# A two-layer trunk of token mixers: the RWKV heads in units of one 128-channel tile, PSUM banks per stage, gate rows through DRAM

## The chip, the cores and the metric

The kernel runs on one core of one Trainium2 chip. The metric is the device time of one execution in microseconds (us); less is better. The core has TensorE (PE, the matrix engine, whose results go to PSUM, eight banks of 128 x 512 fp32), VectorE (DVE), ScalarE (ACT), GpSimd (POOL), and SyncE (SP), whose instruction stream issues all DMA transfers here. Each engine takes its own instructions in a fixed order and waits on semaphores for the others.

## What is computed

Two decoder layers on x (256 tokens x 2048 channels, fp32). Layer 0 mixes tokens with eight mLSTM heads of 128 channels and sixteen RWKV-7 heads of 64; layer 1 with retention and gated DeltaNet (GDN). Each layer has a mixer and a SwiGLU part, both as

```python
shift, scale, gate = _ada(c, ada_w[layer, 0], ada_b[layer, 0])   # silu(c) @ (2048 x 6144), in thirds
h = x * (1.0 + scale) + shift
y = _mixer_ab(h, ...)                       # layer 0; _mixer_cd in layer 1; _swiglu in the second half
x = _layer_norm(ALPHA * x + (1.0 + gate) * y, ln_g[layer, 0], ln_b[layer, 0])
```

The part that the change is about is the RWKV recurrence, for each head with a 64 x 64 state S:

```python
def step(S, inp):
    rt, wt, kt, vt, at, bt = inp                       # at = -kk, bt = kk * a
    sa = jnp.einsum('bhij,bhj->bhi', S, at)
    S = S * wt[:, :, None, :] + sa[..., None] * bt[:, :, None, :] + vt[..., None] * kt[:, :, None, :]
    return S, jnp.einsum('bhij,bhj->bhi', S, rt)
...
y = _head_norm(jnp.moveaxis(y, 0, 1), ln_g, ln_b, eps=RWKV_LN_EPS)
bonus = ((rh * kh * r_k.reshape(H, N)).sum(-1, keepdims=True) * vh).reshape(B, T, -1)
return ((y + bonus) * g).astype(z.dtype)
```

## The kernel before

The program is written in a tile framework: the Python code names tiles from pools, and a scheduler makes each engine's fixed order from program order, priorities, its own estimate of times, and free buffers. A tile is given out when one of its pool's buffers is free.

All large products go through `unit` (lines 360 to 362): a 1 MB block of fp32 weights is loaded into one of three `raw` buffers, ACT and DVE split it into a high and a low part (`split`, lines 340 and 341), and 24 matmuls of 512 columns follow, three for each exact product. `product` joins two to four such units into two of the four `g` banks. Between units, `fill` works off the modulation matrix: for each 1 MB piece of `ada` a DMA into a `raw` buffer and one DVE instruction (line 292). `ada_unit` collects the gates in `g1`; `gate_rows` (line 320) spreads them over 128 partitions with 16 matmuls against the identity, at each of four calls.

The stages in order: start (`first_products`, until about 165 us), RWKV, mLSTM, output product with layer norm (`mix_out`), SwiGLU (`ffn`), and the same for layer 1.

RWKV (`rwkv`) runs four batches of two 128-channel tiles (four heads). `rwkv_tiles` (708) turns a product's result (`zt`, two buffers) to channels by tokens, in `z` tiles (six buffers, three for each 128-channel tile). `rwkv_front` (741 to 778) makes from them the decayed operands `ar` and `bk`. `rwkv_heads` then makes the scores (793, eight blocks of 128 x 512 for each batch: copies by ACT 794, 795 and DVE 796, the triangle by POOL 662), inverts eight triangular 128 x 128 matrices (`inverses`: a DVE loop of 14 steps with a shuffle, a product and a sum, 624 to 626, then three levels of small matmuls, 642, 649, 656), applies the state over the two token blocks (809 to 835), normalizes (840 to 848, with the `rsqrt` of lines 412 to 418), turns the result (853) and multiplies it by the gate (861 to 863) into `yT`. Small fp32 matmuls are two PE records each.

Buffers: `a8` has five of 8 KB a partition (a batch takes two, `mk` and `rbkr`; `yT` takes one for each four tiles; the first products hold one until their tiles are turned), `y8` three (a batch takes two). Small fp32 tiles come from `mix`. Of the PSUM banks four are `g`, three `m` (the first free is taken) and one `c`. mLSTM weights (`mlstm_weights`, 971 to 975) are made for each head with five matmuls, of which two add the running maximum.

Of the kernel before, what the change touches and what calls it, by code (L numbers as in the profile page):

```python
# [10 lines left out]
F32 = mybir.dt.float32  # L11
# [8 lines left out]
P = 128  # L20
T = 256
# [12 lines left out]
LEVELS = (16, 32, 64)  # L34

# [12 lines left out]
for _name, _w in [("ident", 128), ("cum", 256), ("tr", 128), ("ones", 128), ("sl", 128), ("tri", 32), ("diag", 16), ("blk", 8),  # L48
                  ("lev", 64 * len(LEVELS)), ("bones", 128), ("hsel", 2), ("freq", 64)]:
    CONS[_name] = (_n, _w)  # L50
    _n += _w
# [3 lines left out]
def constants():  # L55
# [10 lines left out]
    before = ((u > 63) & (u < t)).astype(np.float64) - ((u <= 63) & (u >= t))  # L66
    put("cum", DECAY * np.concatenate([after, before], 1))
    put("tr", u <= t)
# [120 lines left out]
class Trunk:  # L189
    def __init__(self, tc, ins, out, stack):  # L190
# [11 lines left out]
        self.mix = pool("mix", 1)  # L202
        self.ps_g = pool("psg", 4, space=PSUM)
        self.ps_m = pool("psm", 3, space=PSUM)
        self.ps_c = pool("psc", 1, space=PSUM)
        self.dram = pool("scratch", 1, space=DRAM)
        self.n = 0
# [25 lines left out]
    def f1(self, shape):  # L233
        return self.mix.tile(shape, F32, tag="f1", bufs=3, name=self.name("f"))

# [46 lines left out]
    def ada_unit(self, u, deep):  # L282
# [27 lines left out]
        if i % 4 == 3:  # L310
            v.scalar_tensor_tensor(self.g1[:, i - 35:i - 31], m[:, i - 3:i + 1], 1.0, self.cols[:, ob + i - 3:ob + i + 1], ALU.add, ALU.add)

    def gate_rows(self):

        gate = self.y8([P, D])
        for n in range(4):
            b = self.bank("c")
            for j in range(4):
                k = 4 * n + j
                self.nc.tensor.matmul(b[:, P * j:P * j + P], self.g1[:, k:k + 1].to_broadcast([P, P]), self.ident, start=True, stop=True)  # L320
            self.nc.scalar.activation(gate[:, 512 * n:512 * n + 512], b[:], AF.Copy)
        return gate
# [85 lines left out]
    def rsqrt(self, out, x, shape):  # L408
# [194 lines left out]
    def inverses(self, mt, dd):  # L603
# [4 lines left out]
        d, dt = dd[:, 0], dd[:, 1]  # L608
        halves = [slice(0, 4), slice(4, 8)]
        four = lambda x: x.rearrange("p (h t) -> p h t", h=4)  # L610
        with self.tc.high_priority(offset=4000):
            e2 = self.t1([P, 8, 2, BASE])
            for q in range(4):
# [3 lines left out]
                                self.cons[r, o:o + 32].rearrange("p (a c) -> p a c", a=2).unsqueeze(1).to_broadcast([32, 8, 2, BASE]), ALU.mult)  # L617
            u, e, f = (self.own([P, 8, BASE], "e1", 3) for _ in range(3))
            v.tensor_tensor(u[:], e2[:, :, 0, :], e2[:, :, 1, :], ALU.add)
            v.tensor_tensor(e[:], u[:], self.con("diag").unsqueeze(1).to_broadcast([P, 8, BASE]), ALU.add)  # L620
            for k in range(BASE - 2, 0, -1):
# [3 lines left out]
                v.tensor_tensor(x, x, u[:, :, k:k + 1].to_broadcast([P, 8, n]), ALU.mult)  # L625
                v.tensor_tensor(e[:, :, k + 1:], e[:, :, k + 1:], x, ALU.add)
        for hs in halves:
            v.tensor_tensor(dt[:, hs, :].rearrange("p h (n c) -> p h n c", c=BASE), e[:, hs, :].unsqueeze(2).to_broadcast([P, 4, 8, BASE]),
                            self.con("blk").unsqueeze(1).unsqueeze(3).to_broadcast([P, 4, 8, BASE]), ALU.mult)
            b = self.bank()  # L630
# [4 lines left out]
        for n, size in enumerate(LEVELS):  # L635
# [3 lines left out]
            for hs in halves:  # L639
                x = self.bank()  # L640
# [3 lines left out]
            for x in b:  # L644
                p.append(self.own([P, 4, 64], "P", 2))
                v.tensor_tensor(p[-1][:], four(x[:, 0:256]), mask, ALU.mult)
            for hs, x, y in zip(halves, b, p):
                for j in range(4):
                    nc.tensor.matmul(x[:, 256 + 64 * j:320 + 64 * j], dt[:, hs.start + j, :], y[:, j, :], start=True, stop=True)  # L649
            for hs, x in zip(halves, b):  # L650
                o = dv[:, hs, :, 0, :]
                v.tensor_tensor(o, x[:, 256:512].rearrange("p (h n b) -> p h n b", h=4, b=size), o, ALU.add)
            for hs in halves:
                x = self.bank()
# [3 lines left out]
        return dt  # L658
# [13 lines left out]
    def rwkv_low(self, banks):  # L672
        nc = self.nc
        z = self.q4([P, NT, 288])
        self.g16 = self.fix.tile([P, NT, 16], F32, name="gates")
# [3 lines left out]
        lr = self.q4([P, 3, T])  # L679
        self.lr = lr  # L680
# [34 lines left out]
    def rwkv_batch(self, i):  # L715
# [8 lines left out]
        for t in range(NT):  # L724
# [3 lines left out]
        arbk = self.y8([P, 2, 2, 2, 256])  # L728
        return dict(i=i, w=w, sg=sg, ar=arbk[:, 0].rearrange("p c t (x s) -> p c t x s", x=2),
                    bk=arbk[:, 1].rearrange("p c x (t s) -> p c x t s", t=2), vb=self.q4([P, 2, 2, T]), bkt=self.own([P, 2, 2, P], "b2", 3),  # L730
                    rho=self.tiny([P, NT, 4], "rho", 2), scol=self.tiny([P, 2], "scol", 2))

    def rwkv_front(self, B, c):
        nc, v = self.nc, self.nc.vector
        ct = c % 2
        rm, km, vm = (self.rkv.pop((c, j)) for j in range(3))
        tok = lambda x: x.rearrange("p (t s) -> p t s", t=NT)
        ar, bk, w = B["ar"], B["bk"], B["w"]
        b = self.bank("c")
        for t in range(NT):  # L740
            nc.tensor.matmul(b[:, T * t:T * t + T], B["sg"][:, t, P * ct:P * ct + P], self.con("cum"), start=True, stop=True)
        gg = self.own([P, NT, 2, P], "gg", 1)
        bv = b[:].rearrange("p (t x s) -> p t x s", t=NT, x=2)
        nc.scalar.activation(gg[:], bv, AF.Exp)
        gi = self.f1([P, NT, P])
        nc.scalar.activation(gi[:], bv[:, :, 0, :], AF.Exp, scale=-1.0)
        v.reciprocal(B["scol"][:, ct:ct + 1], gg[:, 1, 1, 0:1])
        v.tensor_tensor(B["scol"][:, ct:ct + 1], B["scol"][:, ct:ct + 1], gg[:, 0, 0, P - 1:P], ALU.mult)
        b = self.bank("c")
        nc.tensor.matmul(b[:, 0:T], w[:64, 1, P * ct:P * ct + P], self.lr[:64, 1, :], start=True, stop=True)  # L750
        a = self.f1([P, T])
        nc.scalar.activation(a[:], b[:, 0:T], AF.Sigmoid, bias=self.col("a0", c))
# [611 lines left out]
```

## Time and profile before

| | |
|---|---|
| median of three runs | 2866.2 us (2865.12 to 2867.47) |
| the profiled execution | 2870.56 us, of which the span from the first to the last instruction is 2868.8 us |
| mean granted TensorE clock | 0.969 of 2.4 GHz |
| busy share of the span | PE 94%, DVE 71%, ACT 44%, POOL 3% |
| moved by DMA | 674 MB, 235 GB/s in the mean |

The profile is of one execution. A busy share is a mean over stages; the clock is 1.0 or 0.5 of full speed in any stretch, and a value between is a mean. Matmuls are pipelined, so that their durations overlap; how long a group holds PE is read from its start to the next group's start. In the granted clock's column 0.69 over 50 us means that the clock was at 1.2 GHz for 31 of them.

### The profile page before, as it was taken

Reading aid. Unit: us, or ns where it says so; the run is one execution under the profiler, and the core shown is the slowest. Engines: PE = TensorE matmul, PEld = TensorE weight load, DVE = VectorE, ACT = ScalarE, POOL = GpSimd, SP = SyncE. Lnnn points to the kernel's source line nnn. Section 1 sums busy time; section 2 is a strip of 40 time slices with the busy share of each in tenths; the row PEclk is TensorE's granted clock in tenths of the full one; section 3 lists DMA queues with packets and bytes.
Section 4 is the critical chain, followed back from the end, with each engine's and each line's share of the span. In section 5 each row is a group of like instructions: output and inputs, shape, how many; then the busy total and the mean of one; then the engine's idle time right before and its main releaser. Section 6 shows DMA issues by size and latency. Waiting matters only on the chain.

```text
span 2868.8 us, 33529 instructions
## 1 busy us (share of the span) xinstructions
PE 2692.8 (94%) x12746; PEld 2215.4 (77%) x12746; DVE 2041.5 (71%) x3255; ACT 1263.7 (44%) x1664; POOL 82.5 (3%) x86
## 2 busy tenths in 40 slices
PE   3699798999899999999998999999989999999997
PEld 2577676777688888888887878787878888888886
DVE  7879677786877557767767898986876545557546
ACT  2264353457354444444444644444444444443442
POOL 0000000011000000000000100101000000000000
PEclk9799798899999999999999999999999999999998
DMA  9977254463568668867855886667656656666553
GB/s 367 354 278 273 92 181 162 181 245 117 197 251 297 249 221 300 301 234 268 298 216 186 296 310 222 247 227 268 222 201 247 235 191 235 235 222 240 193 216 130
DMA packets 106185, 674.34 MB, mean 235 GB/s; under 512 B 12068, under 2 KB 14248, under 8 KB 28328
## 3 DMA queue, kind: packets, MB, share of 16 engines
q1 hardware_dynamic: 106024, 672.20, 64.1%
q8 instruction: 100, 1.64, 0.2%
q14 instruction: 61, 0.50, 0.0%
HBM read 663.77 MB, written 8.39 MB: 234 GB/s over the span
## 4 chain that ended last, share of the span: by engine, by line
PE 77%; DVE 14%; DMA 5%; issue 2%; ACT 2%; POOL 0%; POOLq 0%; SPq 0%; DVEq 0%; ACTq 0%
PE g L361 22%; PE g L362 22%; PE g L360 22%; DVE lo L341 4%; DVE raw L292 4%; DMA raw<-ada 2%; ACT hi L340 1%; PE m L642 1%; PE m L649 1%; DMA raw<-gu 1%; DVE a L292 1%; PE m L793 1%; PE m L578 1%; PE m L656 1%; DMA a<-ada 1%
## 5 line engine op out<-in xcount | busy, mean ns | idle before, releaser
L341 DVE TENSOR_TENSOR lo<-raw,hi 128x1024 fp32r<-128x1024 f32 (+2 forms) x848 | 1022.5, 1211 | 626.4 <-ACT hi L340 623.9
L340 ACT ACTIVATE hi<-raw 128x1024 fp32r<-128x1024 f32 (+2 forms) x848 | 884.4, 1049 | 1164.5 <-PE g L362 931.8
L360 PE MATMUL g<-hi,h 128*128 128x512 f32 (+3 forms) x2368 | 930.0, 395 | 83.4 <-ACT hi L340 77.5
L361 PE MATMUL g<-lo,h 128*128 128x512 f32 (+3 forms) x2368 | 934.5, 395 | 7.4 <-DVE lo L341 7.3
L362 PE MATMUL g<-hi,h 128*128 128x512 f32 (+3 forms) x2368 | 929.8, 393 | 0.0
L360 PEld LDWEIGHTS g<-hi,h 128*128 128x128 f32 x2368 | 452.1, 191 | 178.0 <-ACT hi L340 79.9
L361 PEld LDWEIGHTS g<-lo,h 128*128 128x128 f32 x2368 | 452.5, 191 | 104.0 <-DVE lo L341 16.8
L362 PEld LDWEIGHTS g<-hi,h 128*128 128x128 f32 x2368 | 452.3, 191 | 88.0 <-issue 1.7
L292 DVE SCALAR_TENSOR_TENSOR raw<-raw,silu_c 128x2048 f32<-128x2048 f32 x176 | 405.0, 2302 | 29.7 <-DMA raw<-ada 29.0
L360 PE MATMUL g<-hi,a 128*128 128x512 f32 x960 | 375.2, 391 | 1.1 <-ACT hi L340 1.1
L361 PE MATMUL g<-lo,a 128*128 128x512 f32 x960 | 374.3, 390 | 0.6 <-DVE lo L341 0.6
L362 PE MATMUL g<-hi,a 128*128 128x512 f32 x960 | 374.5, 390 | 0.0
L360 PEld LDWEIGHTS g<-hi,a 128*128 128x128 f32 x960 | 180.2, 188 | 38.5 <-ACT hi L340 1.6
L361 PEld LDWEIGHTS g<-lo,a 128*128 128x128 f32 x960 | 180.3, 188 | 37.8 <-DVE lo L341 0.9
L362 PEld LDWEIGHTS g<-hi,a 128*128 128x128 f32 x960 | 180.2, 188 | 37.0
L918 DVE SCALAR_TENSOR_TENSOR f<-c,cols_sb,f 128x255 f32<-128x255 f32 (+2 forms) x120 | 57.0, 475 | 7.5 <-ACT f L916 6.6
L1115 POOL TENSOR_SCALAR s<-cons_sb,log_alpha 128x128 f32<-128x128 f32 x16 | 18.6, 1177 | 1040.7 <-PE g L362 884.6
L530 ACT ACTIVATE t<-m,affine 128x128 f32<-128x128 f32 x96 | 35.1, 476 | 29.9 <-PE m L527 29.9
L403 ACT ACTIVATE t<-t,affine 128x256 f32<-128x256 f32 x16 | 8.7, 589 | 75.9 <-DVE affine L301 75.9
L292 DVE SCALAR_TENSOR_TENSOR a<-a,silu_c 128x2048 f32<-128x2048 f32 x16 | 36.6, 2287 | 0.4 <-DMA a<-ada 0.3
L527 PE MATMUL m<-cons_sb,y 128*128 128x128 f32 x96 | 16.7, 317 | 18.4 <-DVE v L495 18.4
L662 POOL TENSOR_SCALAR_AFFINE_SELECT a<-a 128x512 f32<-128x512 f32 (+1 forms) x20 | 20.7, 1040 | 454.2 <-ACT a L795 410.1
(386 smaller groups left out, 1966.5 us busy)
## 6 DMA issues: line engine op xcount, KB each, us to landing
raw<-ada SPq DMA_DIRECT2D x176, 1024.0 KB, 5.0
raw<-gu SPq DMA_DIRECT2D x176, 1024.0 KB, 4.9
raw<-dn SPq DMA_DIRECT2D x88, 1024.0 KB, 4.8
raw<-w_cd SPq DMA_DIRECT2D x60, 1024.0 KB, 4.8
raw<-w_ab SPq DMA_DIRECT2D x56, 1024.0 KB, 4.9
a<-ada SPq DMA_DIRECT2D x16, 1024.0 KB, 10.4
raw<-o_ab SPq DMA_DIRECT2D x16, 1024.0 KB, 4.8
raw<-o_cd SPq DMA_DIRECT2D x16, 1024.0 KB, 4.8
```

Source lines behind the costliest of these rows:

```text
L292: v.scalar_tensor_tensor(w[:], w[:], 1.0, self.sc[:], ALU.mult, ALU.mult, accum_out=m[:, i:i + 1])
L340: nc.scalar.activation(hi[:, :2 * n], ws, AF.Copy)
L341: nc.vector.tensor_tensor(lo[:, :2 * n], ws, hi[:, :2 * n], ALU.subtract)
L360: mm(o, ah, wh, start=first, stop=False)
L361: mm(o, ah, wl, start=False, stop=False)
L362: mm(o, al, wh, start=False, stop=stop and k == 3)
L530: nc.scalar.activation(h32[:, j, :], b[:, P * j:P * j + P], AF.Identity, bias=self.ab[:, 16 + k:17 + k], scale=self.ab[:, k:k + 1])
L578: nc.tensor.transpose(b[:, P * k:P * k + P], gs[:, t, P * k:P * k + P], self.ident)
L642: nc.tensor.matmul(x[:, 64 * j:64 * j + 64], mt[:, hs.start + j, :], dv[:, hs.start + j, :, 0, :], start=True, stop=True)
L649: nc.tensor.matmul(x[:, 256 + 64 * j:320 + 64 * j], dt[:, hs.start + j, :], y[:, j, :], start=True, stop=True)
L656: nc.tensor.transpose(x[:, P * j:P * j + P], d[:, hs.start + j, :], self.ident)
L918: v.scalar_tensor_tensor(o[:, d:T], z[:, 0:T - d], self.col(wname, c + 3 - d), o[:, d:T], ALU.mult, ALU.add)
```

## The change

RWKV works in units of one tile (two heads, four matrices). A pair of tiles shares the loads of its small weights, the decay's sigmoid and now that of `a` (`rwkv_pair`). A unit takes one `y8` buffer (`ar`, `bk`, both forms of the inverse), one `a8` buffer (matrix and masked scores) and one `q4` buffer (V, bonus, the turned `bk`), so that three fit. Its scores and inverse use one bank, `m0` or `m1` in turn; its state steps, norm and output use one bank, `s`. One DVE product with a constant mask of 384 columns takes the place of a copy by ACT, a copy by DVE and the POOL triangles. The `cum` constant has 129 columns in place of 256. The products' order is set by `NEED`. `inverses` takes four or eight matrices. Banks belong to two stages (`banks`): `m0`, `m1`, `s`, `c` up to the end of the first mixer, where a general `bank()` takes `m0`, `m1` and `s` in turn, and then three `m` and `c` as before. The `mix` pool is closed and opened again at that border, and tiles that were kept for good (gates, cos, sin and others) lie in it. `gate_rows` is now a DMA: when the last gate is known, the 16 columns are turned with one transpose, stored to DRAM, and read back as a row for all partitions. The mLSTM gates carry the differences of the running maximum, so that a head's weights need four matmuls of 128 columns. A step of `rsqrt` has three instructions in place of four.

```diff
+NEED = (3, 3, 3, 4, 5, 5, 6, 6)
-    put("cum", DECAY * np.concatenate([after, before], 1))
-    put("tr", u <= t)
+    put("cum", DECAY * np.concatenate([-(u <= 63).astype(np.float64), after], 1))
+    put("m3", np.concatenate([u <= t, u < t, u <= t], 1))
...
     def bank(self, kind="m"):
-        return {"g": self.ps_g, "c": self.ps_c, "m": self.ps_m}[kind].tile([P, 512], F32, tag=kind, name=self.name(kind))
+        if kind == "m" and kind not in self.ps:
+            self.turn = (self.turn + 1) % 3
+            kind = ("m0", "m1", "s")[self.turn]
+        pool = self.ps_g if kind == "g" else self.ps[kind]
+        return pool.tile([P, 512], F32, tag=kind, name=self.name(kind))
+    @contextmanager
+    def banks(self, **kinds):
+        with ExitStack() as st:
+            self.ps = {k: st.enter_context(self.tc.tile_pool(name=self.name("ps" + k), bufs=n, space=PSUM)) for k, n in kinds.items()}
+            self.mix = st.enter_context(self.tc.tile_pool(name=self.name("mix"), bufs=1))
+            yield
...
-        if i % 4 == 3:
-            v.scalar_tensor_tensor(self.g1[:, i - 35:i - 31], m[:, i - 3:i + 1], 1.0, self.cols[:, ob + i - 3:ob + i + 1], ALU.add, ALU.add)
+        if i == 47:
+            v.scalar_tensor_tensor(self.g1[:], m[:, 32:48], 1.0, self.cols[:, ob + 32:ob + 48], ALU.add, ALU.add)
+            b = self.bank("c")
+            nc.tensor.transpose(b[:16, 0:P], self.g1[:], self.ident)
+            row = self.t1([16, P])
+            nc.scalar.activation(row[:], b[:16, 0:P], AF.Copy)
+            self.gate_row = self.dram.tile([16, P], F32, name=self.name("gate_row"))
+            nc.sync.dma_start(self.gate_row[:], row[:])
     def gate_rows(self):
         gate = self.y8([P, D])
-        for n in range(4):
...
+        self.nc.sync.dma_start(gate[:], self.gate_row[:].rearrange("k p -> (k p)").unsqueeze(0).to_broadcast([P, D]))
         return gate
...
-            v.tensor_tensor(t[:], out, out, ALU.mult)
+            v.scalar_tensor_tensor(t[:], out, -0.5, out, ALU.mult, ALU.mult)
             v.tensor_tensor(t[:], t[:], x, ALU.mult)
-            v.tensor_scalar(t[:], t[:], -0.5, 1.5, ALU.mult, ALU.add)
-            v.tensor_tensor(out, out, t[:], ALU.mult)
+            v.scalar_tensor_tensor(out, t[:], 1.5, out, ALU.add, ALU.mult)
...
+    def rwkv_scores(self, B):
+        lane = str(B["c"] % 2)
+        x8 = self.a8([P, 2048])
+        mt = x8[:, 0:512].rearrange("p (j s) -> p j s", j=4)
+        rk = B["rk"] = x8[:, 512:].rearrange("p (j x s) -> p j x s", j=4, x=3)
...
+                b = self.bank("m" + lane)
+                for x in range(2):
+                    nc.tensor.matmul(b[:, T * x:T * x + T], B["bk"][r, x, t, :], B["ar"][r, t].rearrange("p x s -> p (x s)"), start=True, stop=True)
+                nc.scalar.activation(mt[:, j, :], b[:, 0:P], AF.Copy, scale=B["rho"][:, t, h:h + 1])
+                v.tensor_tensor(rk[:, j], b[:, P:4 * P].rearrange("p (x s) -> p x s", x=3), mask, ALU.mult)
+        self.inverses(mt, B["d"], B["dt"], lane)
+    def rwkv_states(self, B):
+        bank = self.bank("s")
+        xb, xs, yb = bank[:, 0:P], bank[:, P:2 * P], bank[:, 2 * P:4 * P]
...
+        b = self.bank("s")
+        g = b[:, T:2 * T]
...
-        for i in range(4):
-            while len(tokens) < (3, 3, 5, 6)[i]:
+        for c in range(8):
+            while len(tokens) < NEED[c]:
...
+            if c % 2 == 0:
+                pair = self.rwkv_pair(c // 2)
...
+            B = self.rwkv_front(pair, c)
+            self.rwkv_scores(B)
+            self.rwkv_states(B)
...
-        mm(b[:, 0:T], L[:, 0, :], tro, start=True, stop=False)
-        mm(b[:, P:T], self.lf[:, 1, h:h + 1].to_broadcast([P, P]), tr, start=False, stop=False)
-        mm(b[:, 0:T], e, self.mneg[:], start=False, stop=True)
-        mm(b[:, T:T + P], L[:, 1, :], tr, start=True, stop=False)
-        mm(b[:, T:T + P], e, self.mneg[:, P:T], start=False, stop=True)
+        mm(b[:, 0:P], L[:, 0, :], tr, start=True, stop=True)
+        mm(b[:, P:T], L[:, 0, :], self.con("ones"), start=True, stop=False)
+        mm(b[:, P:T], self.lf[:, 1, h:h + 1].to_broadcast([P, P]), tr, start=False, stop=True)
+        mm(b[:, T:T + P], L[:, 1, :], tr, start=True, stop=True)
...
+        with k.banks(m0=1, m1=1, s=1, c=1):
...
+            k.mixer_ab(h, 48.0 / 44, early)
+        with k.banks(m=3, c=1):
+            x, h = k.mix_out(ins["o_ab"], x, 0)
```

## Rows read from the trace of the kernel before

**Rows 1.** The page: busy time of the engines (share of the span, instructions), and the granted TensorE clock in 40 equal slices of the span.

```profile
PE 2692.8 (94%) x12746; PEld 2215.4 (77%) x12746; DVE 2041.5 (71%) x3255; ACT 1263.7 (44%) x1664; POOL 82.5 (3%) x86
...
PEclk9799798899999999999999999999999999999998
```

**Rows 2.** Busy time by stretches of 50 us from 150 to 750 us: stretch and its length, then busy us (instructions) of PE, PEld (weight loads), DVE, ACT and POOL, the granted clock, the DMA share and GB/s. The last row is the sum.

```profile
150.00:200.00 50.00, 49.88 (x229) 39.21 (x228) 38.56 (x53) 32.55 (x49) 0.00 (x0) 1.00 0.75 277
200.00:250.00 50.00, 48.22 (x219) 36.55 (x218) 45.58 (x92) 28.36 (x48) 4.99 (x5) 1.00 0.76 280
250.00:300.00 50.00, 48.28 (x300) 41.60 (x299) 42.84 (x93) 20.62 (x29) 0.00 (x0) 1.00 0.66 244
300.00:350.00 50.00, 35.59 (x143) 26.10 (x143) 29.92 (x124) 19.81 (x48) 3.93 (x5) 0.69 0.17 57
350.00:400.00 50.00, 50.00 (x339) 44.70 (x338) 34.81 (x82) 22.60 (x37) 0.00 (x0) 1.00 0.45 162
400.00:450.00 50.00, 42.51 (x178) 30.72 (x177) 42.72 (x119) 24.25 (x50) 6.15 (x5) 0.90 0.59 215
450.00:500.00 50.00, 42.69 (x303) 38.27 (x301) 35.48 (x91) 19.23 (x32) 0.00 (x0) 0.97 0.39 137
500.00:550.00 50.00, 46.56 (x179) 33.87 (x180) 38.71 (x107) 23.07 (x47) 4.05 (x6) 0.84 0.41 154
550.00:600.00 50.00, 49.92 (x328) 44.60 (x327) 36.82 (x70) 20.05 (x35) 0.00 (x0) 0.98 0.61 214
600.00:650.00 50.00, 46.16 (x199) 35.00 (x198) 41.94 (x95) 26.63 (x41) 15.90 (x14) 0.94 0.74 275
650.00:700.00 50.00, 49.96 (x249) 40.35 (x248) 31.87 (x84) 34.87 (x53) 4.93 (x8) 0.96 0.30 106
700.00:750.00 50.00, 46.99 (x217) 37.00 (x216) 37.20 (x85) 27.28 (x39) 1.27 (x3) 1.00 0.49 168
sum 600.00, PE 556.76 PEld 447.97 DVE 456.46 ACT 299.32 POOL 41.23; mean PE 46.40 PEld 37.33 DVE 38.04 ACT 24.94 POOL 3.44
```

**Rows 3.** The timeline between the first batch and the second: start, duration, engine, line, operation, tiles and shapes, count, and in brackets the idle time of the engine before it with what ended it. Between the first of these rows and the last there is no product matmul (360 to 362).

```profile
295.17 0.48 PE L362 MATMUL g<-hi,h 128*128 128x512 f32 x1
...
315.43 2.48 ACT L848 ACTIVATE t<-m,v,v 128x64 f32<-128x64 f32 x8 [12.02 <-DVE v L845]
...
316.19 0.47 PE L853 MATMUL m<-cons_sb,t 128*128 128x128 f32 x1 [7.97 <-ACT t L848]
...
319.54 2.40 PE L793 MATMUL m<-y 64*128 64x256 f32 x6
...
339.05 0.80 PE L360 MATMUL g<-hi,h 128*128 128x512 f32 x1 [1.05 <-ACT zt L698]
```

**Rows 4.** The timeline at the ends of what follows the inverses (state steps, norm, output), of the first batch and of the fourth: its first matmul and its last product with the gate.

```profile
294.14 0.56 PE L810 MATMUL m<-q,a 128*128 128x64 f32 x4
...
324.27 0.43 DVE L863 TENSOR_TENSOR s<-m,s 128x256 f32<-128x256 f32 x1 [1.63 <-PE m L862]
...
574.85 1.00 PE L810 MATMUL m<-q,a 128*128 128x64 f32 x8
...
619.35 0.42 DVE L863 TENSOR_TENSOR s<-m,s 128x256 f32<-128x256 f32 x1 [0.62 <-PE m L862]
```

**Rows 5.** Groups of DVE instructions by line and shape from 150 to 700 us: count, busy us, mean ns of one, idle before. Line 624 is the shuffle of the loop in `inverses`, 616 its first product, 796 the copy of the scores, 1013 the product of the mLSTM scores (from PSUM), 417 a step of `rsqrt`.

```profile
L796 DVE COPY a<-m 128x256 f32<-128x256 f32 x32 | 13.1, 420 | 8.4 <-ACT a L795 8.3
...
L616 DVE TENSOR_TENSOR s<-a,cons_sb 32x256 f32<-32x256 f32 x16 | 8.1, 506 | 0.4 <-ACT a L794 0.2
...
L1013 DVE SCALAR_TENSOR_TENSOR t<-m,t 128x384 f32<-128x384 f32 x5 | 2.8, 558 | 9.3 <-POOL t L662 9.2
...
L417 DVE TENSOR_SCALAR v<-v 128x8 f32<-128x8 f32 x15 | 2.5, 167 | 0.2
...
L624 DVE STREAM_SHUFFLE e<-e 128x112 f32<-128x112 f32 x4 | 1.2, 294 | 0.0
...
L624 DVE STREAM_SHUFFLE e<-e 128x56 f32<-128x56 f32 x4 | 0.9, 219 | 0.0
...
L624 DVE STREAM_SHUFFLE e<-e 128x8 f32<-128x8 f32 x4 | 0.7, 179 | 0.0
```

**Rows 6.** The timeline of PE around small matmuls: eight records of `gate_rows` and what follows, and one head of `mlstm_weights` (971 to 975) with the scores that follow.

```profile
690.84 1.06 PE L320 MATMUL c<-cons_sb,one_and_gate 128*128 128x128 f32 x8
691.65 0.48 PE L360 MATMUL g<-hi,a 128*128 128x512 f32 x1
...
702.32 0.60 PE L971 MATMUL m<-cons_sb,s 128*128 128x256 f32 x2
702.75 0.38 PE L972 MATMUL m<-cons_sb,log_f 128*128 128x128 f32 x2
703.07 0.69 PE L973 MATMUL m<-minus_m,cons_sb 8*128 8x256 f32 x2
...
704.52 0.70 PE L985 MATMUL m<-y 128*128 128x256 f32 x2
```

**Rows 7.** DMA issues over the whole span (KB each, median us from issue to landing), and SyncE in the timeline from 683 to 760 us: four loads of x for the residual.

```profile
x<-y SPq DMA_DIRECT2D x24, 256.0 KB, 2.9
t<-lnrow SPq DMA_DIRECT2D x24, 256.0 KB, 4.4
...
703.49 11.98 SPq L440 DMA_DIRECT2D t<-x  x4
```

More of the change, by code (lines that the diff above doesn't have):

```diff
@@ L3 @@
 import math
-from contextlib import ExitStack
+from contextlib import ExitStack, contextmanager
 import numpy as np
@@ L638, in inverses @@
             b, p = [], []
-            for hs in halves:
-                x = self.bank()
+            for hs in parts:
+                x = self.bank("m" + lane)
                 for j in range(4):
@@ L674, in rwkv_low @@
         z = self.q4([P, NT, 288])
-        self.g16 = self.fix.tile([P, NT, 16], F32, name="gates")
+        self.g16 = self.own([P, NT, 16], "g16", 1)
         for t in range(NT):
@@ L727, in rwkv_batch @@
         nc.scalar.activation(sg[:], b[:].rearrange("p (t c) -> p t c", t=NT), AF.Sigmoid)
[L728 to L733, printed above, removed]
+        b = self.bank("c")
@@ L734, in rwkv_front @@
+        a = self.own([P, 2, T], "b2", 3)
+        for j in range(2):
+            nc.tensor.matmul(b[:, T * j:T * j + T], w[:64, 1, P * j:P * j + P], self.lr[:64, 1, :], start=True, stop=True)
+            nc.scalar.activation(a[:, j], b[:, T * j:T * j + T], AF.Sigmoid, bias=self.col("a0", 2 * i + j))
+        return dict(w=w, sg=sg, a=a)
+    def rwkv_front(self, pair, c):
         nc, v = self.nc, self.nc.vector
-        ct = c % 2
+        cs = slice(P * (c % 2), P * (c % 2) + P)
         rm, km, vm = (self.rkv.pop((c, j)) for j in range(3))
@@ L737, in rwkv_front @@
         tok = lambda x: x.rearrange("p (t s) -> p t s", t=NT)
-        ar, bk, w = B["ar"], B["bk"], B["w"]
+        eight = self.y8([P, 4, 512])
+        ar = eight[:, 0].rearrange("p (t x s) -> p t x s", t=NT, x=2)
+        bk = eight[:, 1].rearrange("p (x t s) -> p x t s", t=NT, x=2)
+        four = lambda x: x.rearrange("p (j s) -> p j s", j=4)
+        vb = self.q4([P, 3, T])
+        rho, scol = self.tiny([P, NT, 2], "rho", 3), self.tiny([P, 1], "scol", 3)
         b = self.bank("c")
         for t in range(NT):
-            nc.tensor.matmul(b[:, T * t:T * t + T], B["sg"][:, t, P * ct:P * ct + P], self.con("cum"), start=True, stop=True)
@@ L742, in rwkv_front @@
-        gg = self.own([P, NT, 2, P], "gg", 1)
-        bv = b[:].rearrange("p (t x s) -> p t x s", t=NT, x=2)
+            nc.tensor.matmul(b[:, (P + 1) * t:(P + 1) * (t + 1)], pair["sg"][:, t, cs], self.con("cum"), start=True, stop=True)
+        gg = self.own([P, NT, P + 1], "gg", 1)
+        bv = b[:, 0:NT * (P + 1)].rearrange("p (t s) -> p t s", t=NT)
         nc.scalar.activation(gg[:], bv, AF.Exp)
         gi = self.f1([P, NT, P])
-        nc.scalar.activation(gi[:], bv[:, :, 0, :], AF.Exp, scale=-1.0)
@@ L747, in rwkv_front @@
[L747 to L752, printed above, removed]
+        nc.scalar.activation(gi[:], bv[:, :, 1:P + 1], AF.Exp, scale=-1.0)
+        v.reciprocal(scol[:], gg[:, 1, 0:1])
```

301 lines of the change are left out of this document (135 added, 166 removed).

## The prediction

> **What bounds the kernel now.** I read the page first [rows 1]: PE is busy for 94% of the span, DVE for 71%, and the granted clock falls below full speed in a handful of slices only. A busy PE at full clock can be made shorter only by taking matmuls away; a PE that waits or runs at 1.2 GHz can also be helped by order. So the second view is the table by stretches [rows 2], and in it I multiply PE's busy time by the granted clock: what is missing to 50 us I call lost. From 150 to 750 us, stretch by stretch, 0.1, 1.8, 1.7, 25.4, 0, 11.7, 8.6, 10.9, 1.1, 6.6, 2.0 and 3.0 us are lost, 73 us of 600. Most of it (57 us) lies in the four stretches 300 to 350 and 400 to 550. The third view shows what those are [rows 3]: seams between two RWKV batches. After 295.17 us no product runs until 339.05; PE works through the first batch's state steps, stands 7.97 us before the transposes of 853, because ACT's normalization stood 12.02 us behind DVE's small norm steps, and starts the next batch's scores (793) only at 319.54, after that batch's output has begun. At 339.05 the product starts again behind ACT's copy into `zt`.
>
> The reason stands in the code. A batch holds two `a8` buffers (`mk`, `rbkr`) and two `y8` buffers. Of five `a8`, up to two are held by `yT` and one by the early products; so the next batch's scores wait for the last batch's state steps, and the batches run as one chain. The products that could fill the seam have run ahead until both `zt` buffers and the `g` banks were full, and `zt` comes free only when RWKV takes tiles on. The start before 150 us and the stages behind 750 us are touched only by the gate rows and the shorter `rsqrt`.
>
> **The change part by part.** The sum is made against the profiled execution, 2870.6 us with a span of 2868.8; the median of the runs is 2866.2, 4.4 lower, and I carry the difference over.
>
> *Gate rows.* Eight records hold PE for 691.65 - 690.84 = 0.81 us [rows 6]. A call has four such groups, 3.24 us; in its place comes one transpose, two records, 0.2 us. Four calls in stretches where PE is nearly full: -3.0 each, -12.1 us, of which 3.0 fall before 750 us. The new path is DVE, a transpose in bank `c`, ACT, a store and a load of 1 MB. The store is bounded by the 2.9 us of the stores of x, the load by the 4.4 us of a quarter as much from `lnrow` [rows 7]; the first use of the gate is the residual, behind one product or more, so some 15 us of chain are hidden. SyncE has to wait for ACT before the store, and the weight loads behind it wait too; with three `raw` buffers ahead I take 0, at most 3 us for each call.
>
> *mLSTM weights.* A head holds PE for 704.52 - 702.32 = 2.20 us; a pair of records of 128 columns takes 703.07 - 702.75 = 0.32 there [rows 6], 0.20 in the gate rows' group. Four such pairs, with room for their waits 0.37 each, make 1.48: -0.7 for each of eight heads, -5.8. The gates get four more transposes, +0.8. Together -5.0 (-3 to -7).
>
> *`cum`.* Sixteen fp32 matmuls lose half their columns, at 0.20 us for 128 columns: at most -3.2, at least 0; I take -2.5.
>
> So PE has 10.5 us less work before 750 us and 9.1 us less behind it, about -20 us whatever the order does.
>
> *More DVE work.* Two inverses of four matrices replace one of eight. The loop has 14 steps of three instructions; at 8 to 112 columns they take 179 to 294 ns, at 4 to 56 columns up to 219 [rows 5]. With the middles, 236 and 199 ns, a call costs 9.9 before and 8.4 after, and there are twice as many: +6.8 for each batch, +27. The first products (616, 506 ns at 256 columns) I set at 380 ns for half the width: +4. The masked scores take 558 ns (the row of 1013 has their shape) in place of 420: 32 times, +4.4. The norm has 13 small steps for each of eight units in place of 16 for each of four batches: 40 more at 167 ns, +6.7. Half-wide state products add 1. Together +43 us (bounds +30 and +55), so that DVE goes from 456 to about 500 us for the same work [rows 2]. ACT loses 32 copies and some table loads; it is at half load and I count nothing. POOL's triangles fall off; nothing waited for them but the state steps.
>
> *The order.* A unit takes one `a8` and one `y8` buffer, so three are in work: while one unit is in its norm, the next is in its inverse, and a third in its front. That is what fills the seams. How much of the 73 us comes back is the one large unknown. After the change the stage has 600 - 73 - 10.5 = 516.5 us of PE work and 500 us of DVE work: two engines loaded alike. The stretches in which DVE is at 41.9 us of 50 or more lose 1.8, 1.7, 11.7 and 6.6 us [rows 2]: from 3.5% in the two best to 11% in the mean. On a stage of some 550 us that is 19 to 60 us. I take 37, nearer the middle, since neither the undisturbed stretches nor those with a seam in them are like the new stage. The stage takes 516.5 + 37 = 553.5 us, 46.5 less; DVE is then at 90%.
>
> *The border of the stages.* `mix` is closed and opened again, so the loads of x for the residual may wait until the last mLSTM tile is done. They stand on SyncE ahead of weight loads; before, four of them already held it for 11.98 us [rows 7]. I take +3 us, with 0 and +12 as ends.
>
> Sum: -46.5 - 9.1 + 3 = -52.6, from 2870.6 to 2818 and on the scale of the median 2813.6. Forecast: 2814 us.
>
> **The rivals.** *DVE takes the place of the seam.* With 500 us of work and in-order waits for PSUM, DVE may hold every chain: an older unit's small norm steps then stand behind pieces of `ada` and splits, as in the first seam, and 60 to 73 us stay lost. Then 2837 to 2850. For it: 43 us more work on an engine at 76% in this stage. Against it: from 200 to 300 us DVE is at 88% and PE loses 3.5 us.
>
> *One bank for all state work: slower.* Everything behind the inverses of every unit passes through the single bank `s`, one unit at a time. Before, that part took 324.70 - 294.14 = 30.6 us in the first batch and 619.77 - 574.85 = 44.9 in the fourth [rows 4], and three banks let neighbours overlap. Eight units of S us must fit into the 325.6 us from 294.14 to 619.77, or some 375 if the first unit gets there 50 us earlier: the break lies at S = 41 to 47. Half the matmuls, statistics and scalings of a batch make me expect 24 to 34, which fits. But if DVE's queue stretches it to 50 us, the stage ends 24 us later than before with nothing left to run beside it, and 2866.2 - 19.6 + 24 + 3 gives about 2874, up to 2890 at 52 us. The seams' rows speak for the mechanism, the halved work against. The Trainium skill (Perfetto Trace Analysis, Matmuls) says that independent matmul groups should rotate through different PSUM banks, so that one group's evacuation runs beside the next group's matmuls; the change does the opposite inside a unit, and by that rule this case, and the slow lanes of the scores, would be the likely one. No row here shows a single bank held so.
>
> *Nearly all comes back.* The chains of three units fill each other as the stretches from 200 to 300 us do, 10 to 20 us stay lost: 2787 to 2797.
>
> *It does not get three in work.* `q4` has five buffers for two `w` and three `vb`, `z` six for two tiles: if these hold the third unit back, two overlap. The seams halve at best: 50 us lost, 2827.
>
> **How the numbers follow.** Forecast (25 to 50 us lost, 2802 to 2827) 0.45; DVE in the seam's place 0.25; the single bank, slower, 0.12; nearly all back 0.13; two in work 0.05. The range leaves out half of the slow case and the ends of the others, with the terms' own bounds: 2784 to 2857. A measurement of this kernel tells about 0.2% from no change, 5.7 us. Faster 0.82, the same 0.08 (the mild end of the slow case and the far end of the DVE case), slower 0.10.
>
> **What would show it.** The gate rows' matmuls are gone and nothing waits for the store. In the table by stretches from 150 us on, PE's busy time times clock should miss 2 to 5 us in each 50, with no stretch of 25, and DVE should stand at 44 to 47 of 50 in the RWKV part. Scores of unit c + 1 should start before unit c's norm, and the part behind the inverses should take 24 to 34 us a unit. The first tokens of `mix_out`'s layer norm should come some 45 us earlier. It is wrong if state steps stand in a row behind bank `s` for over 41 us each, if PE still has stretches without products, or if the loads of x hold the weights back at the border.

## The result, and the profile after

The changed kernel takes 2878.3 us in the median of seven runs (2872.5 to 2884.6), the kernel before 2866.6 in seven runs beside it: ratio 1.0044, 95% interval 1.0032 to 1.0055. It is 0.44% slower; the forecast was 2814 us. The profiled execution took 2877.5 us, with a span of 2875.8.

The page, busy time and granted clock by slices, which answers to [rows 1]:

```profile
PE 2705.0 (94%) x12610; PEld 2217.9 (77%) x12610; DVE 2055.3 (71%) x3518; ACT 1246.2 (43%) x1614; POOL 61.9 (2%) x76
...
PEclk9799589989999999999999999999999999999998
```

136 PE instructions are gone, and yet PE is busy for 12 us more: the fifth slice stands at half clock. The table by stretches, with the columns of [rows 2]:

```profile
150.00:200.00 50.00, 50.00 (x224) 39.21 (x223) 38.68 (x49) 29.21 (x42) 0.00 (x0) 1.00 0.79 289
200.00:250.00 50.00, 49.77 (x218) 36.45 (x217) 45.66 (x124) 23.06 (x37) 0.00 (x0) 1.00 0.80 285
250.00:300.00 50.00, 46.58 (x255) 38.96 (x254) 41.39 (x125) 19.61 (x28) 0.00 (x0) 0.93 0.63 232
300.00:350.00 50.00, 44.97 (x146) 32.50 (x144) 25.60 (x126) 11.20 (x29) 0.45 (x3) 0.50 0.13 44
350.00:400.00 50.00, 47.89 (x250) 40.00 (x250) 29.87 (x124) 19.25 (x37) 0.00 (x0) 0.75 0.14 47
400.00:450.00 50.00, 49.52 (x257) 38.91 (x257) 42.95 (x157) 22.34 (x38) 0.41 (x2) 1.00 0.55 194
450.00:500.00 50.00, 49.05 (x289) 38.85 (x289) 39.45 (x128) 23.34 (x43) 0.20 (x1) 1.00 0.48 170
500.00:550.00 50.00, 45.72 (x218) 34.80 (x217) 42.40 (x176) 18.62 (x30) 0.32 (x2) 0.86 0.44 155
550.00:600.00 50.00, 49.96 (x297) 41.69 (x296) 36.14 (x102) 19.80 (x31) 0.20 (x1) 1.00 0.63 227
600.00:650.00 50.00, 35.47 (x157) 28.24 (x156) 33.20 (x69) 25.17 (x46) 13.04 (x21) 0.76 0.41 150
650.00:700.00 50.00, 47.69 (x231) 39.73 (x230) 45.23 (x94) 35.09 (x49) 0.73 (x1) 0.97 0.75 281
700.00:750.00 50.00, 49.67 (x247) 40.56 (x246) 41.63 (x91) 34.75 (x49) 1.23 (x3) 1.00 0.56 193
```

50 us less PE's busy time times clock, summed, gives 87.8 us lost, where the kernel before lost 73. From 400 to 500 us the change does what was hoped: 1.4 us are lost there in place of 20.3. From 300 to 350 PE looks busy (45 of 50), but at half clock and on small matmuls alone; no product runs, and DMA falls to 44 GB/s. Two places hold most of the loss, 288 to 371 and 605 to 631 us (45 and 19 us).

The first, in the timeline (columns as in [rows 3], to which it answers): the last product before it, the end of the second unit's gate product, then what had to come before the next product.

```profile
288.49 0.39 PE L378 MATMUL g<-hi,h 128*128 128x512 f32 x1
...
347.38 1.22 PE L867 MATMUL s<-lr,q 32*128 32x256 f32 x2
...
348.63 0.33 SPq L733 DMA_DIRECT2D q<-lw  x1
...
352.73 2.02 PE L738 MATMUL c<-q,lr 65*128 65x256 f32 x4
...
360.96 1.22 PE L744 MATMUL c<-lr,q 64*128 64x256 f32 x2
...
363.87 1.06 PE L721 MATMUL c<-cons_sb,zt 128*128 128x128 f32 x4
...
367.99 1.06 PE L721 MATMUL c<-cons_sb,zt 128*128 128x128 f32 x4
...
369.46 1.08 ACT L711 ACTIVATE zt<-g 128x512 f32<-128x512 f32 x2
370.67 0.77 PE L376 MATMUL g<-hi,h 128*128 128x512 f32 x1
```

Read it from the end. The product waits for its banks until ACT has copied the last result into `zt` (711); both `zt` buffers are full until the fourth block is turned (721); in program order the turning stands behind the third pair's small matmuls (738, 744), on PE and in bank `c`; their weights are loaded (733) when a `q4` buffer comes free, and that is when the second unit's gate product (866, 867) has read the first pair's weights, 0.03 us before the load.

The second place: the path of the gate row. Turned columns (328), ACT's copy (330), the store (332), and the first mLSTM convolution's transposes (922), which need bank `c` too; then the same in the second mixer.

```profile
511.70 0.28 PE L328 MATMUL c<-cons_sb,one_and_gate 128*16 128x128 f32 x1
...
606.82 0.25 ACT L330 ACTIVATE s<-c 16x128 f32<-16x128 f32 x1
...
611.71 0.42 SPq L332 DMA_DIRECT2D gate_row<-s  x1
...
612.25 1.06 PE L922 MATMUL c<-cons_sb,zt 128*128 128x128 f32 x4
...
1683.45 0.28 PE L328 MATMUL c<-cons_sb,one_and_gate 128*16 128x128 f32 x1 [0.73 <-DVE one_and_gate L326]
...
1739.95 0.25 ACT L330 ACTIVATE s<-c 16x128 f32<-16x128 f32 x1
1740.25 0.42 PEld L922 LDWEIGHTS c<-cons_sb,zt 128*128 128x128 f32 x4 [0.39 <-ACT s L330]
```

The columns stand in `c` for 95 us and for 56.5 us, because the copy waits for a `t1` tile. In the first case it comes free only when the tiles ahead of it in the program, the last unit's states and output, are done with. RWKV's triangles on POOL and the gate rows' 16 matmuls are gone; DVE's groups of the new parts, from 150 to 800 us (columns as in [rows 5]), and the last output product (873) of the units, first and last start:

```profile
L639 DVE STREAM_SHUFFLE e<-e 128x4 f32<-128x4 f32 (+6 forms) x112 | 21.4, 191 | 0.1
L641 DVE TENSOR_TENSOR e<-e,e 128x4 f32<-128x4 f32 (+6 forms) x112 | 20.8, 186 | 1.2
L640 DVE TENSOR_TENSOR e<-e,e 128x4 f32<-128x4 f32 (+6 forms) x112 | 20.8, 185 | 1.1
L814 DVE TENSOR_TENSOR a<-m,cons_sb 128x384 f32<-128x384 f32 x32 | 17.7, 554 | 6.5 <-ACT a L813 6.4
```

```profile
L873 DVE TENSOR_TENSOR s<-s,s x8: 415/422/425, 309.9 to 604.9; 128x256 f32<-128x256 f32 x8
```

Eight units end 42 us apart. In [rows 4] the four batches ended from 324.27 to 619.35, 98 us apart, so two units take 84 us for a batch's 98.

How far the first mixer as a whole has moved shows in the first stores behind its layer norm (SyncE's issues of `y` to `x`): of the kernel before, of the changed kernel, and of the kernel with three edits that comes below.

```profile
L537 SPq DMA_DIRECT2D x<-y x8: 319/328/398, 782.7 to 788.5; - x8
```

```profile
L552 SPq DMA_DIRECT2D x<-y x8: 319/332/1017, 794.9 to 800.6; - x8
```

```profile
L552 SPq DMA_DIRECT2D x<-y x8: 319/327/379, 742.8 to 748.5; - x8
```

The changed kernel is 12 us late there, and 7 us at the end of its span.

### The profile page after: what moved, and what is told of

Its sections match the earlier page's. It is cut to its first block, busy times and chain, and to the rows that moved or that the text cites. A ratio compares the mean times of both kernels' runs of the same rounds, so it can differ in the third digit from the quotient of the medians.

```text
span 2875.8 us, 33431 instructions
## 1 busy us (share of the span) xinstructions
PE 2705.0 (94%) x12610; PEld 2217.9 (77%) x12610; DVE 2055.3 (71%) x3518; ACT 1246.2 (43%) x1614; POOL 61.9 (2%) x76
## 4 chain that ended last, share of the span: by engine, by line
PE 81%; DVE 11%; DMA 4%; ACT 2%; issue 1%; POOL 0%; POOLq 0%; SPq 0%; DVEq 0%; ACTq 0%
PE g L377 23%; PE g L378 23%; PE g L376 23%; DVE lo L357 3%; DVE raw L307 3%; DMA raw<-ada 2%; PE m L812 1%; PE m L664 1%; PE m L657 1%; DVE a L307 1%; PE m L593 1%; DMA t<-x 1%; ACT hi L356 1%; PE m L671 1%; DMA a<-ada 1%
## 5 line engine op out<-in xcount | busy, mean ns | idle before, releaser
L812 PE MATMUL m<-y 64*128 64x256 f32 x128 | 48.7, 496 | 6.3 <-DVE a L814 3.2
L1131 POOL TENSOR_SCALAR s<-cons_sb,gl 128x128 f32<-128x128 f32 x16 | 20.5, 1296 | 1050.2 <-PE g L378 886.7
L812 PEld LDWEIGHTS m<-y 64*128 64x128 f32 x128 | 25.2, 227 | 20.8 <-issue 8.3
```

Of the source, the lines that this page charges most:

```text
L812: nc.tensor.matmul(b[:, T * x:T * x + T], B["bk"][r, x, t, :], B["ar"][r, t].rearrange("p x s -> p (x s)"), start=True, stop=True)
```

## The experiments

All ratios are to the kernel before, run beside each. The gain of an edit is the difference of its median to the 2878.3 us of the changed kernel, where no other is named.

**The gate row's buffer.**

```diff
-            row = self.t1([16, P])
+            row = self.f1([16, P])
```

> One line of the change is altered: the 16 x 128 tile into which ACT copies the turned gate columns comes from the tag f1 and not from t1. In the changed kernel the turned columns stand in bank c from 512 to 607 us, because the copy waits for a t1 buffer, and all four t1 buffers go through the state steps of the units. Theory A (this holds the convolutions of mLSTM, which need bank c, and with them the products): the copy comes right behind 512 us, the first convolution's transposes come at 515 to 530 and not at 612, the stretch from 600 to 650 us loses about 7 us in place of 23, and the second such hold, 1683 to 1740 us in the second mixer, goes too, which gives back its 8 us: 2850 to 2862 us. Theory B (the stretch from 605 to 631 us is the chain of the mLSTM gates, whose small DVE steps end at 611.6, and the convolution would wait for them on TensorE anyway): 2874 to 2880 us, with the convolution still behind 605.

It takes 2856.4 us, ratio 0.9963 (0.9950 to 0.9975): 22 us less than the changed kernel, as theory A said. The timeline, and its stretch from 600 us:

```profile
504.95 0.28 PE L328 MATMUL c<-cons_sb,one_and_gate 128*16 128x128 f32 x1
505.32 0.25 ACT L330 ACTIVATE f<-c 16x128 f32<-16x128 f32 x1
...
505.77 0.60 PE L922 MATMUL c<-cons_sb,zt 128*128 128x128 f32 x4
```

```profile
600.00:650.00 50.00, 45.91 (x214) 36.64 (x213) 44.73 (x88) 28.23 (x44) 13.71 (x15) 0.97 0.79 286
```

The convolution starts 106 us earlier, 5.5 us are lost there in place of 23, and the hold in the second mixer shrinks from 56.5 to 2.1 us. The first seam, too, ends 8 us earlier (363 us); the traces don't show why.

**The turning ahead of the pair's weights.**

```diff
-            if c % 2 == 0:
-                pair = self.rwkv_pair(c // 2)
             while 4 * made < 3 * c + 3:
                 self.rwkv_tiles(tokens[made], made)
                 made += 1
+            if c % 2 == 0:
+                pair = self.rwkv_pair(c // 2)
```

> The turning of the product tiles stands ahead of the pair's small weights in the program, not behind them. In the changed kernel no product runs from 288 to 371 us, because both zt buffers are full until the fourth block is turned at 364 to 369, and that stands behind the third pair's matmuls (353 to 362), whose weights wait for a q4 buffer until 349. The z buffers for the block are free at about 304 us, when the fourth unit's front has read its tiles. Theory A (the order on TensorE and bank c starves the products): the turning comes at 305 to 315 us, the product starts again by 320 and the time at half clock in this seam falls from 82 us to 45 or less; 2848 to 2862 us. Theory B (the fronts and the inverses set the pace and the products only follow): the seam moves, the mixer ends where it did, 2872 to 2882 us.

It takes 2854.3 us, 0.9958 (0.9943 to 0.9973): 24 us less, theory A. The fourth block:

```profile
304.77 0.49 PE L721 MATMUL c<-cons_sb,zt 128*128 128x128 f32 x3
...
320.44 0.66 PE L721 MATMUL c<-cons_sb,zt 128*128 128x128 f32 x4
...
321.50 1.08 ACT L711 ACTIVATE zt<-g 128x512 f32<-128x512 f32 x2
...
343.09 0.33 SPq L733 DMA_DIRECT2D q<-lw  x1
```

The weights still come at 343 us, but the fourth block's turning no longer waits for them. The stretch from 300 to 350 us loses 6.5 us in place of 27.5.

**The gate product in the front.**

```diff
-        vb = self.q4([P, 3, T])
+        vb = self.q4([P, 4, T])
...
+        b = self.bank("c")
+        nc.tensor.matmul(b[:, 0:T], pair["w"][:, 2, cs], self.lr[:, 2, :], start=True, stop=False)
+        nc.tensor.matmul(b[:, 0:T], pair["w"][64:96, 1, cs], self.lr[64:96, 1, :], start=False, stop=True)
+        nc.scalar.activation(vb[:, 3], b[:, 0:T], AF.Copy)
...
-        v.tensor_tensor(o[:], g, o[:], ALU.mult)
+        v.tensor_tensor(o[:], B["g"], o[:], ALU.mult)
```

> The gate product of a unit is made in its front, in bank c, and copied into a fourth quarter of the unit's q4 tile, so that a pair's weights are done with after the second front and not after the second unit's output. Two copies of 256 columns by ACT for a pair are added, no arithmetic is altered. Theory A (the rival of the forecast that q4 holds the third unit back): the third pair's weights are loaded at about 310 us, when the first unit's output frees its buffer, not at 349; the turning of the fourth block and the product follow at 315 to 325, the half clock of the seam falls from 82 us to about 45, and at times three units are between front and output: 2845 to 2862 us. Theory B (y8, of which each unit takes one buffer from its front to its output, holds the third unit as well): the fronts stay at the times that they have (275, 304, 375, 409), 2868 to 2880 us.

It takes 2862.0 us, 0.9988 (0.9978 to 0.9997): 16 us less, at the very end of theory A's range. The third pair's weights are loaded at 308 us, right behind the first unit's output. The fourth block is turned from 332 us and the product follows at 344, later than theory A's 315 to 325. The hold of the gate row is still there, with the columns in `c` from 491 to 592 us, and 29.1 us are lost from 550 to 600.

**`ar`, `bk` of a pair in one `y8` tile, its inverses in another.**

```diff
-        eight = self.y8([P, 4, 512])
+        arbk = pair["arbk"][:, c % 2]
...
+        if B["c"] % 2 == 0:
+            B["pair"]["dd"] = self.y8([P, 2, 2, 512])
```

> The decayed operands of both units of a pair share one y8 tile and the inverses of both another, as a batch had it before; all else is as in the changed kernel. Theory A (a unit's y8 buffer, taken at its front and held to its output, keeps the fronts from running ahead): the fronts of the third and fourth unit come at 225 to 260 us, not at 275 and 304, their scores follow one another without a stop, and the seam at 288 to 371 us shrinks by 20 us or more: 2850 to 2865 us. Theory B (the third pair's weights in q4, or the order on bank c, hold the products): the fronts come earlier, but the product still stops from about 290 to 350 or more: 2872 to 2884 us.

It takes 2872.4 us, 1.0030 (1.0017 to 1.0043). The fronts stay at 275 and 304 us, and the next product comes at 364: the theory that `y8` holds the fronts back fell, and theory B, too, had expected them earlier.

**The small matmuls alone, on the kernel before.** Its batches are kept; `gate_rows`, `ada_unit`'s last lines, `cum`, `rsqrt`, `mlstm_gates` and `mlstm_weights` are those of the change, with the gate row's tile in `f1`.

> The kernel before, with its batches, buffers and banks, and only the smaller matmuls of the change: the gate rows through DRAM (with the ACT copy's tile in f1), the mLSTM gates and weights with four matmuls a head, the narrower cum constant, the shorter rsqrt. Theory A (these terms stand by themselves: about 20 us of TensorE work goes, as the changed kernel's trace shows, and what the change loses is all in the units' order): 2842 to 2852 us, ratio about 0.993. Theory B (the work taken away was under other waits, or the gate's way over DRAM brings waits of its own): 2858 us or more.

It takes 2856.3 us, 0.9963 (0.9944 to 0.9982): some 10 us less than the kernel before, between the two theories. PE has 136 records fewer. An estimate from the matmul records: taken at their shape's step to the next at full clock (0.11 us for 128 columns, 0.215 for 256), they held PE for 21 us or somewhat more, about as forecast. But the stretches from 150 to 750 lose 84 us in place of 73: with less small work the seams are wider, for which no run gives the reason.

**Both orders, then all three edits.**

> The changed kernel with both orders mended: the gate row's tile in f1, and the turning of the product tiles ahead of the pair's weights. Each gave 22 to 24 us by itself. Theory A (two separate stalls, one at 288 to 371 us and one at 605 to 631 with its like in the second mixer): the gains add, 2828 to 2838 us. Theory B (both act on the same end of the RWKV stage, where DVE's work sets the length): little is added, 2846 to 2856 us.

It takes 2841.2 us, 0.9914 (0.9897 to 0.9930), between the theories: of the 46 us that the two give by themselves, 37 are left. The same kernel with the early gate product as well was measured twice:

> As the kernel with both orders mended, and the gate product made in the front as well, so that a pair's weights leave q4 after the second front. Theory A (q4 still holds the third unit back): units end every 36 to 38 us, three are between front and output, lost TensorE time from 150 to 750 us falls to 40 us or less, 2818 to 2830 us. Theory B (once the turned tiles come early, the pace is set by DVE or by y8): 2828 to 2840 us, as without it.

> The same kernel as with all three edits (gate row's tile in f1, turning ahead of the pair's weights, gate product in the front), with more rounds, beside the next one. Theory A (its gain of 1.5% is real): ratio 0.983 to 0.988 and 2817 to 2828 us. Theory B (the four runs behind it were partly chance, as their spread from 2819 to 2833 us allows): ratio above 0.988.

It takes 2819.9 us, 0.9851 (0.9825 to 0.9877), and 2819.1, 0.9830 (0.9807 to 0.9853). This beats both kernels, the one before by 45 and 49 us, and both theories A come out in time. Its two stretches around the old seam, and its units' ends:

```profile
300.00:350.00 50.00, 47.43 (x217) 37.10 (x217) 34.18 (x144) 20.92 (x40) 0.41 (x2) 0.76 0.38 134
350.00:400.00 50.00, 49.98 (x300) 40.87 (x299) 40.45 (x139) 21.29 (x40) 0.20 (x1) 1.00 0.45 169
```

```profile
L874 DVE TENSOR_TENSOR s<-q,s x8: 401/418/422, 305.3 to 600.0; 128x256 f32<-128x256 f32 x8
```

The units still end 42 us apart, where theory A had 36 to 38 (and 40 us lost or less). What changed is what runs beside them: 41.6 us are lost from 150 to 750 in place of 87.8.

**The banks.** Both runs have the gate row's tile in `f1` and compare with its 2856.4 us. With three banks in turn for everything in the first stage:

```diff
-        if kind == "m" and kind not in self.ps:
-            self.turn = (self.turn + 1) % 3
-            kind = ("m0", "m1", "s")[self.turn]
+        if kind in ("m0", "m1", "s"):
+            kind = "m"
...
-        with k.banks(m0=1, m1=1, s=1, c=1):
+        with k.banks(m=3, c=1):
```

> The kernel with the gate row's tile in f1, and in the first stage three banks for all small work in turn, as before the change, in place of one bank for each lane of scores and inverses and one for the states. Theory A (a bank of its own for each lane makes every step of a lane wait for the copy out of the last one; the rule that independent groups should rotate through banks holds here): scores and levels of one unit run closer, 2835 to 2850 us. Theory B (the lanes' banks cost nothing, since the other lane and the products fill TensorE, and the seam has other reasons): 2852 to 2862 us, as with one bank each (2856).

Or with the lanes' two banks in turn and `s` by itself (`m=2, s=1, c=1`; one bank of the first products moves to `s`):

> The changed kernel with the gate row's tile in f1, and the two lanes' banks made one pool of two that scores and inverses of all units take in turn; the states keep their own bank. With three banks in turn for everything the kernel took 2980 us, and units ended 60 to 87 us apart. Theory A (a pool hands out its banks in program order, so that a unit's scores wait for the last banks of the unit before, which its inverse holds): units' scores stand behind the last unit's inverse, 2870 to 2940 us, between the two. Theory B (it was the states' long hold on a bank of the shared pool alone): 2850 to 2862 us, as with a bank for each lane. Theory C (rotating helps, as it lets a copy out of one bank run beside the matmuls into the other): below 2848 us.

They take 2980.0 us, 1.0399 (1.0382 to 1.0415), and 2910.6, 1.0148 (1.0128 to 1.0168). Neither theory of the first had a loss; the second is theory A. The units' ends, first of three banks, then of two:

```profile
L872 DVE TENSOR_TENSOR s<-m,s x8: 411/422/425, 298.1 to 770.1; 128x256 f32<-128x256 f32 x8
```

```profile
L872 DVE TENSOR_TENSOR s<-s,s x8: 411/425/425, 295.1 to 691.7; 128x256 f32<-128x256 f32 x8
```

They end 67 and 57 us apart. The program's pools give out their banks in program order, so that a unit's first scores wait for banks that the unit before holds in its inverse or its states. The second unit's scores run from 269 to 283 and from 264 to 273 us, behind the first unit's inverse; with a bank for each lane they run from 230 to 245.

**DVE's load.** On the kernel with all three edits, the `ada` pieces are first moved to another stage, then shortened. The first:

```diff
-        self.rwkv(h, rate, early)
+        self.rwkv(h, 0.0, early)
...
-            self.mlstm_group(g, self.ins["w_ab"], h, rate)
+            self.mlstm_group(g, self.ins["w_ab"], h, 1.5)
```

> The kernel with all three edits, and the pieces of the modulation matrix (2.3 us of DVE each, about one for each product unit) taken out of the RWKV products and spread over the mLSTM products instead, 1.5 for each unit; nothing is left out. Some 13 pieces, 30 us of DVE work, leave the stretch from 165 to about 540 us. Theory A (once the orders are mended DVE's queue is what holds the chains, the second rival of the forecast): the units come every 36 us in place of 43 and 5 to 15 us are won, 2806 to 2816 us. Theory B (the units wait for one another's buffers and for the chain of small steps, not for DVE's throughput; and the pieces, put into mLSTM, hold that): 2816 to 2835 us.

It takes 2833.0 us, 0.9881 (0.9861 to 0.9901), 14 us more. It doesn't test what it should: mLSTM's products run ahead into RWKV and bring the pieces along. Line 307 takes 2.5 us in place of 35.8 from 165 to 300 us, but 68.4 in place of 44.4 from 300 to 540. The first unit ends 44 us earlier (261.4), the last 9.

The second multiplies 48 pieces over 256 of their 2048 columns only. It leaves out seven eighths of that work, so its output is not the reference's; it serves for the time alone.

```diff
-        v.scalar_tensor_tensor(w[:], w[:], 1.0, self.sc[:], ALU.mult, ALU.mult, accum_out=m[:, i:i + 1])
+        n = 256 if 32 <= u < 80 else D
+        v.scalar_tensor_tensor(w[:, :n], w[:, :n], 1.0, self.sc[:, :n], ALU.mult, ALU.mult, accum_out=m[:, i:i + 1])
```

> The kernel with all three edits, in which 48 pieces of the modulation matrix (those that run beside the first mixer) are multiplied over 256 of their 2048 columns only, so that the scales of the first output product and of the SwiGLU behind it are not those of the reference; the loads stay whole. Each piece's two records take about 0.3 us of DVE in place of 2.3, so that some 90 us of DVE work leave the stretch from 150 to 750 us, 18% of its load there, and nothing takes their place. Theory A (with the orders mended DVE's throughput is what is left of the second rival): the 42 us that TensorE still loses there fall to 20 or less, 2785 to 2800 us. Theory B (what is left are chains and buffers, DVE's queue only delays them a little): 2808 to 2822 us.

It takes 2811.1 us, 0.9798 (0.9770 to 0.9825), which overlaps with the 0.9807 to 0.9853 of the whole pieces: theory B. From 150 to 750 us DVE works 434 us in place of 496. The units' ends:

```profile
L875 DVE TENSOR_TENSOR s<-q,s x8: 404/416/426, 265.1 to 505.5; 128x256 f32<-128x256 f32 x8
```

Units come every 34 us and RWKV ends 95 us earlier, but the kernel gains at most some 8 us. PE still loses 31.9 us from 150 to 750, after 41.6: its work there is products for the most part, and earlier units don't make them fewer.

## Why the prediction was wrong

**The order: the step that failed.** The prediction said that three units are in work, that this is what fills the seams, and that of 73 us only 37 stay lost. 87.8 were lost. Three units and more were in work inside the seam:

```profile
303.54 1.07 PE L762 MATMUL c<-cons_sb,b 128*128 128x129 f32 x4
...
304.40 1.06 PE L866 MATMUL s<-lr,q 128*128 128x256 f32 x2
...
307.02 1.81 PE L657 MATMUL m<-y,a 128*128 128x64 f32 x8
...
308.76 2.07 PE L812 MATMUL m<-y 64*128 64x256 f32 x4
```

These are the fourth unit's front (762), the first unit's gate product (866), the second's inverse (657) and the third's scores (812). So the overlap came, and the step from it to filled seams failed: the units' small matmuls went on, at half clock, and the products that were to run beside them were stopped. The rival "It does not get three in work" named the buffer, and with the wrong effect: `q4` held back the third pair's weights, not the third unit. I gave it 0.05 and priced it at 50 us lost, by halving the seams. What I missed is where the blocked instruction stands: ahead of the turning, on which the products hang. Two edits that each take one link away show it: the turning ahead (-24 us) and the early gate product (-16 us).

**Gate rows: the second step that failed.** I listed the transpose in bank `c` and ACT's copy, and counted SyncE's wait, 0 to 3 us a call. The copy's wait for a `t1` tile, and who needs `c` meanwhile, I put at nothing; it is the 22 us of the first experiment, of which the stretch from 600 us shows 17.5. The chain of the mLSTM gates on DVE, the other suspect for that place, is not it: with the tile in `f1` it ends at 627 us, later than before, and the convolution does not wait for it.

**Fewer small matmuls: right on PE, not in time.** The forecast was -19.6 us, the estimate from the records is 21 or more, and on the kernel before it gave 10. "Whatever the order does" was wrong: the seams took half of it back. The saving on the heads was priced too low: four pairs take 0.81 to 0.91 us at full clock in the kernel with three edits (a pair every 0.22), not 1.48.

**More DVE work: the right kind, somewhat less.** The loop takes 63.0 / 8 = 7.9 us a unit, forecast 8.4; the masked scores 554 ns, forecast 558. Summed over the durations of all instructions, the inverses take 141 us in place of 114, and scores, states and `rsqrt` 73 in place of 65: +35 us, where the sum had +43. The page's busy time rises by only 14 us, since durations of neighbouring instructions overlap (2236 us summed, 2055 busy). In the kernel with three edits DVE is at 83% from 150 to 700 us, where 90% was forecast.

**DVE in the seam's place (0.25).** Not the cause: DVE is busy for 25.6 and 29.9 us of 50 in the stretches of the first seam and for 33.2 in that of the second, and edits that leave its work as it is give back 59 us. It does set the units' pace, 42 against 34 us, and that hardly reaches the end.

**One bank for state work (0.12).** Not the cause either: from the first product with the inverse (833) to the output product (873) a unit takes 22 to 43 us, 30 in the mean, near the 24 to 34 foreseen. `s` does pass from unit to unit within 4 us, but only the fourth unit's inverse (ready at 401) had to wait for it (405). The slower sign and the time, inside its 2874 to 2890, came out as in this rival by luck, through other mechanisms. The Trainium skill (Perfetto Trace Analysis, Matmuls) says that independent matmul groups should rotate through different PSUM banks. Here rotation inside one pool cost 54 and 124 us against a bank for each lane. My reading, which no run tests, is that the other lane and the products already give what the rule wants, matmuls beside a copy.

**The border.** +3 us forecast; the stretch from 750 to 800 loses 11.3 us (42.57 us busy at 0.91), 11.7 before. No loss shows there.

**What is left.** Of the 64 us between forecast and measurement the three edits give back 59: 2819 us against 2814. Behind the first mixer the kernel with three edits gains 8 us on the one before (its first stores come 40 us earlier, its span is 48 us shorter), where the gate rows' share was 9.1. That 41.6 us are lost, against 37, is in part chance, since 11.2 of them lie in the layer norm from 700 us, behind the stage that the forecast meant. Of the others 10.1 lie from 600 to 650 us, with their cause open, and 14.0 from 300 to 350. In that stretch the fourth block is still turned only behind the fourth unit's front:

```profile
311.25 1.11 PE L721 MATMUL c<-cons_sb,zt 128*128 128x128 f32 x4 [0.47 <-ACT q L798]
```

The wait that ended last is for bank `c`, out of which ACT has just copied that unit's gate product (798). No run takes this link away by itself.

## What to carry to other kernels

When a change adds a step, follow every buffer that it waits for and every one that it holds meanwhile: a 0.25 us copy waiting for a small tile held a single bank for 95 us. When a rival says that a buffer holds a unit back, look at what stands behind the waiting instruction on its engine before pricing it. Here, where pools hand out in program order, chains that should overlap did better with banks of their own.

## What the runs showed of the hardware

From 300 to 350 us TensorE was busy for 45 of 50 us, with small matmuls only and no product, at a granted clock of 0.50 (1.2 GHz); the four transposes of 128 columns at 364 us took 421 ns each and came 0.21 us apart, and the four at 174 us, at full clock, 272 or 273 ns and 0.11 us. So this seam cost twice: the products that didn't run, and the units' matmuls, which took twice as long. A busy share of 90% hid it; the clock's column and GB/s showed it.
